# Two transformer blocks on one core: the rounded half of every weight tile is written by ScalarE instead of GpSimd

## The chip, the cores and the metric

The kernel runs on one core of a Trainium2 chip. The metric is the device time of one execution in microseconds (us); the time of a kernel is the median of several runs. The engines are TensorE (PE in the profile; PEld is its loading of weights), VectorE (DVE), ScalarE (ACT), GpSimd (POOL) and SyncE (SP), which here issues most of the DMA transfers.

## The reference

The input `x` is 1 x 1024 tokens x 1024 channels in fp32. Two blocks follow each other:

```python
# block 1
h = rms_norm(x, norm1_g)
q, k, v, g_ret, u, g_s5 = split(h @ w_in)
ret = retention(rotary(q), rotary(k), v) * silu(g_ret)     # 8 heads, chunks of 128
ssm = s5_branch(u) * silu(g_s5)      # linear recurrence, gelu, then
                                     # y * sigmoid(y @ glu_w + glu_b)   (the GLU)
x = x + concat(ret, ssm) @ w_out
x = x + cross_attention(rms_norm(x), rms_norm(mem)) @ xa_wo   # 256 memory tokens
x = rms_norm(x, norm_f_g)
# block 2
p = rmsnorm(x) @ w_in_2
x = x + concat(sgu, short_conv, delta_rule, gla)(p) @ w_out_2
x = x + (silu(h @ w_gate) * (h @ w_up)) @ w_down       # h = rmsnorm(x), 2816 hidden
out = rmsnorm(x, final_norm_w_2)
```

All of it must have fp32 accuracy.

## The kernel before

**Split operands.** TensorE multiplies in a rounded format (`float32r`). To keep fp32 accuracy each operand a is held as two tiles: `hi`, which is a rounded to that format, and `lo` = a − hi, exact. A product of two matrices is then three matmuls into the same PSUM accumulator (`mm3`, L187 to L189): hi·hi, hi·lo and lo·hi. So every weight tile that comes from memory must be split before TensorE can use it, and every activation too.

**A weight tile** is 128 input channels x 8 k-tiles x 128 output columns, seen by an engine as 128 partitions x 1024 elements, 512 KB. `weights()` (L169) issues its DMA on SP into `wraw` (three buffers), writes `whi` (four buffers) and then `wlo` (four buffers). `wlo` on VectorE (L182) reads `wraw` and `whi`, so it always follows the rounding. 204 tiles go this way. Activations are split by `split()` (L164): hi always on ScalarE (L166), lo on VectorE or GpSimd (L167).

**The projections.** `gproj()` (L191) walks over the output tiles of a projection. For each it multiplies 8 k-tiles x 3 matmuls = 24 matmuls of 128 x 512 into one of three PSUM buffers (`mm`), and then calls `evac`, which takes the result from PSUM. With one tile to a group the weights are loaded two tiles ahead. What `evac` does differs by stage; much of it is on ScalarE.

**Stages that the change's neighbours are in** (us of the span of the profiled execution):
- 0 to 110: the start. The memory is normalized, its keys and values are projected and written to DRAM (`ka_d`, `va_d`, through ScalarE copies `mo`, L166), and x is turned and normalized.
- 194 to 303: the S5 inputs. For each of 8 channel tiles four complex products are made; in each, one product is on VectorE and one (`m`, L1398) on GpSimd, and VectorE adds the two (`W`, `E`, L1403). TensorE transposes W (L1422). Projections run beside it.
- 318 to 350: the retention of block 1 begins; ScalarE issues a DMA that fills a DRAM buffer with zeros (`t_d`, L1116), then goes on taking results of projections from PSUM (`g` L480, `sg` L1141).
- 690 to 812: the S5 outputs go to DRAM and come back turned (`oy` L1095, `y_d`).
- 837 to 935: the GLU's projection. `evac` of one tile is a chain through four engines (quoted below); its buffers `sig`, `yt` and `yo` exist once each, so the next tile's L557 and L555 wait for this tile's L560.
- 1214 to 1300: the first block's last two norms beside the last projection. Squares are summed on GpSimd (`ssq`, L274; the squares `sq` come from ScalarE), and TensorE's column sum `ms` (L280) waits for them; GpSimd also scales x (L995) and splits (L311).
- 1950 to 2500: gate/up and down projections of the SwiGLU. Gate and up are done by Winograd's seven products, whose weights are sums and differences of weight tiles, split in `prep()` (L768). There the rounding is on ScalarE for the first pair of tiles and on GpSimd for the other 21.

```python
# evac of the GLU (L555 to L561, shortened)
nc.scalar.activation(sig, ps, AF.Sigmoid, bias=gb[:, ct:ct + 1])      # L555
nc.gpsimd.tensor_add(t, y[0][:, ct], y[1][:, ct])                     # L557  yt
nc.gpsimd.tensor_mul(t, t, sg)                                        # L558  yt
nc.vector.tensor_mul(o, t, sig)                                       # L560  yo
self.split(dst[0][:, ct], dst[1][:, ct], o)                           # L166 ACT, L167 DVE
```

**What sets the order.** The program is built with `tile.TileContext(nc, schedule_with_timeline_sim=True)` (L2211): a scheduler decides by its own model of times in which order each engine's instructions stand in its queue; an engine then runs its queue strictly in that order. Only SP in the start stage and TensorE in the early part of gate/up keep the order of the code.

## Time and profile before

| what | value |
|---|---|
| median of 3 runs | 2550.29 us |
| lowest, highest run | 2542.23, 2551.26 us |
| profiled execution, first to last instruction (span) | 2543.1 us |
| profiled execution, its own time outside of the profile | not listed apart; its span lies 0.9 us above the fastest run |
| mean granted TensorE clock of the profiled execution | 0.985 |

The profile is of one execution. A time in it stands in us from the span's start. Since its span lies at the fastest of the three runs, and two of the runs took 8 to 9 us more, a change that is read from the profile is to be added to the median as a difference.

### The profile page before, as it was taken

How to read it: one execution, taken by the hardware profiler on the slowest of the kernel's cores; microseconds unless marked ns; L12 is line 12 of the kernel's file. 1: busy time of each engine (PE TensorE's matmuls, PEld its weight loads, DVE VectorE, ACT ScalarE, POOL GpSimd, SP SyncE). 2: the span in 40 equal slices, each digit the busy share in tenths (PEclk: the TensorE clock that was granted, in tenths of full speed). 3: DMA queues.
4: the chain of work that ended last, by engine and by line, in shares of the span. 5: the costliest groups of instructions: out<-in, count | busy, mean ns of one | idle time of the engine just before them, and what ended most of it. 6: DMA issues, size and time to landing. Idle time of an engine off the chain costs nothing.

```text
span 2543.1 us, 34912 instructions
## 1 busy us (share of the span) xinstructions
PE 2432.7 (96%) x13241; PEld 2030.9 (80%) x13241; DVE 1589.5 (63%) x2722; ACT 553.2 (22%) x981; POOL 1021.7 (40%) x905
## 2 busy tenths in 40 slices
PE   7998889999999989999999999999989999999998
PEld 7886679999977768888777688977868888888886
DVE  6456669934523765544776653357688766667777
ACT  4223300000001211233343211144240101010002
POOL 4226513423411676436855632145454433321002
PEclk9999999999999999999999999999999999999999
DMA  8745462112697343553336464246243222234222
GB/s 246 222 98 159 149 121 67 60 43 82 214 297 215 119 124 113 169 182 100 93 112 193 132 182 140 83 135 217 82 132 109 92 79 88 84 105 177 99 100 83
DMA packets 421383, 336.81 MB, mean 132 GB/s; under 512 B 46848, under 2 KB 364752, under 8 KB 420384
## 3 DMA queue, kind: packets, MB, share of 16 engines
q1 hardware_dynamic: 378960, 291.05, 37.5%
q10 hardware_dynamic: 42256, 43.52, 6.0%
q8 instruction: 105, 1.72, 0.3%
q14 instruction: 62, 0.51, 0.1%
HBM read 239.00 MB, written 95.52 MB: 132 GB/s over the span
## 4 chain that ended last, share of the span: by engine, by line
PE 73%; POOL 8%; DVE 7%; DMA 5%; issue 5%; SPq 1%; ACT 1%; ACTq 1%; POOLq 0%; DVEq 0%
PE mm L187 18%; PE mm L189 17%; PE mm L188 17%; PE qkv L187 3%; PE qkv L188 2%; PE qkv L189 2%; POOL m L1398 2%; POOL whi L181 1%; PE yps L1089 1%; POOL yt L558 1%; POOL yt L557 1%; POOL ssq L274 1%; PE yps L1085 1%; DVE wlo L182 1%; DMA y<-y_d 1%
## 5 line engine op out<-in xcount | busy, mean ns | idle before, releaser
L187 PE MATMUL mm<-s,whi 128*128 128x512 f32 (+1 forms) x2112 | 837.7, 399 | 28.5 <-ACT sg L1141 9.3
L189 PE MATMUL mm<-s,wlo 128*128 128x512 f32 (+1 forms) x2112 | 829.5, 393 | 5.4 <-DVE wlo L773 4.9
L188 PE MATMUL mm<-s,whi 128*128 128x512 f32 (+1 forms) x2112 | 828.8, 393 | 3.6 <-POOL s L311 2.0
L187 PEld LDWEIGHTS mm<-s,whi 128*128 128x128 f32 x2112 | 402.8, 191 | 121.1 <-issue 17.5
L181 POOL TENSOR_SCALAR whi<-wraw 128x1024 fp32r<-128x1024 f32 x204 | 248.7, 1222 | 618.3 <-PE mm L188 318.0
L189 PEld LDWEIGHTS mm<-s,wlo 128*128 128x128 f32 x2112 | 403.1, 191 | 90.8 <-DVE wlo L773 6.4
L188 PEld LDWEIGHTS mm<-s,whi 128*128 128x128 f32 x2112 | 403.6, 191 | 84.8 <-POOL s L311 3.7
L182 DVE TENSOR_TENSOR wlo<-wraw,whi 128x1024 fp32r<-128x1024 f32 x204 | 297.6, 1461 | 127.7 <-POOL whi L181 126.8
L868 DVE TENSOR_TENSOR s<-mm,s 128x512 f32<-128x512 f32 x176 | 117.4, 686 | 67.0 <-PE mm L189 66.9
L187 PE MATMUL mm<-whi,s 128*128 128x512 f32 (+1 forms) x416 | 155.3, 373 | 1.5 <-DVE mo L167 1.5
L188 PE MATMUL mm<-wlo,s 128*128 128x512 f32 (+1 forms) x416 | 155.1, 373 | 0.5 <-DVE wlo L182 0.5
L189 PE MATMUL mm<-whi,s 128*128 128x512 f32 (+1 forms) x416 | 154.5, 373 | 0.0
L187 PE MATMUL qkv<-whi,s 128*128 128x256 f32 x512 | 151.5, 296 | 0.0
L188 PE MATMUL qkv<-wlo,s 128*128 128x256 f32 x512 | 147.1, 288 | 0.0
L189 PE MATMUL qkv<-whi,s 128*128 128x256 f32 x512 | 146.9, 287 | 0.0
L274 POOL TENSOR_TENSOR ssq<-ssq,sq 128x512 f32<-128x512 f32 x56 | 91.3, 1641 | 28.2 <-ACT sq L273 27.4
L770 POOL TENSOR_SCALAR whi<-wraw 128x1024 fp32r<-128x1024 f32 (+1 forms) x60 | 59.1, 988 | 108.2 <-PE mm L188 79.7
L187 PEld LDWEIGHTS qkv<-whi,s 128*128 128x128 f32 x512 | 97.3, 190 | 4.7 <-issue 3.9
L289 POOL TENSOR_TENSOR rs<-rv,mhalf 128x4 f32<-128x4 f32 (+3 forms) x47 | 52.3, 1115 | 114.2 <-DVE rv L287 113.8
L188 PEld LDWEIGHTS qkv<-wlo,s 128*128 128x128 f32 x512 | 97.4, 190 | 0.9
L189 PEld LDWEIGHTS qkv<-whi,s 128*128 128x128 f32 x512 | 97.4, 190 | 0.3
L739 POOL TENSOR_TENSOR c<-c,c 128x512 f32<-128x512 f32 x44 | 64.3, 1463 | 72.4 <-DVE c L754 43.9
(503 smaller groups left out, 3887.0 us busy)
## 6 DMA issues: line engine op xcount, KB each, us to landing
wraw<-in_w_in_dram SPq DMA_DIRECT2D x58, 512.0 KB
wraw<-in_w_out_dram SPq DMA_DIRECT2D x48, 512.0 KB
wraw<-in_w_gate_up_dram SPq DMA_DIRECT2D x48, 512.0 KB
ff_d<-c SPq DMA_DIRECT2D x44, 256.0 KB
fraw<-ff_d SPq DMA_DIRECT2D x22, 512.0 KB
wraw<-in_w_down_dram SPq DMA_DIRECT2D x22, 512.0 KB
s<-ret_d SPq DMA_DIRECT2D x16, 512.0 KB
s<-x_d SPq DMA_DIRECT2D x16, 512.0 KB
```

Source lines behind the costliest of these rows:

```text
L181: nc.gpsimd.tensor_scalar(hi, raw, 1.0, 0.0, op0=ALU.mult, op1=ALU.add)
L182: nc.vector.tensor_sub(lo, raw, hi.bitcast(F32))
L187: mm(ps, ah, bh, start=start, stop=False)
L188: mm(ps, ah, bl, start=False, stop=False)
L189: mm(ps, al, bh, start=False, stop=stop)
L274: self.nc.gpsimd.tensor_add(ssq, ssq, t)
L289: nc.gpsimd.tensor_tensor(r, v, self.mhalf[:, :1].to_broadcast([P, n]), op=ALU.pow)
L557: nc.gpsimd.tensor_add(t.rearrange("p t c -> p (t c)"), y[0][:, ct].bitcast(F32), y[1][:, ct].bitcast(F32))
L739: g.tensor_mul(src, src, sg[n])
L770: g.tensor_scalar(d[0][:, s], src, 1.0, 0.0, op0=ALU.mult, op1=ALU.add)
L868: v.tensor_add(x, ps, x)
L1398: eng.tensor_tensor(out, a, b, op=ALU.mult)
```

## The change

Three places that rounded a weight tile on GpSimd with `tensor_scalar` (x 1.0 + 0.0) now round it on ScalarE with an `activation` of the function Copy: `weights()` (204 instructions, 128x1024), the inner `split` of `prep()` (102 instructions that were on GpSimd: 39 of 128x1024, 63 of 128x512) and `small_weights()` (1 instruction). Together 307 instructions go from GpSimd's queue to ScalarE's. The lo halves stay on VectorE, and no DMA, matmul or buffer is added or removed. Comments were deleted too, and since three lines of `prep()` go, lines behind L770 carry a number smaller by 3.

```diff
@@ weights()
         hi = self.wp.tile([P, nk, ncol], F32R, tag="whi", name=self.nm("whi"), bufs=4)
         lo = self.wp.tile([P, nk, ncol], F32R, tag="wlo", name=self.nm("wlo"), bufs=4)
-        nc.gpsimd.tensor_scalar(hi, raw, 1.0, 0.0, op0=ALU.mult, op1=ALU.add)
+        nc.scalar.activation(hi, raw, AF.Copy)
         nc.vector.tensor_sub(lo, raw, hi.bitcast(F32))
@@ prep(), inner split
-                if i:
-                    g.tensor_scalar(d[0][:, s], src, 1.0, 0.0, op0=ALU.mult, op1=ALU.add)
-                else:
-                    act.activation(d[0][:, s], src, AF.Copy)
+                act.activation(d[0][:, s], src, AF.Copy)
                 v.tensor_sub(d[1][:, s], src, d[0][:, s].bitcast(F32))
@@ small_weights()
-        nc.gpsimd.tensor_scalar(hi, raw, 1.0, 0.0, op0=ALU.mult, op1=ALU.add)
+        nc.scalar.activation(hi, raw, AF.Copy)
         nc.vector.tensor_sub(lo, raw, hi.bitcast(F32))
```

GpSimd's queue in the GLU's projection, before. A row is the line, the operation, what it writes and reads, and its shape; `s` and `sgl` are the two halves and the gate of the S5 output.

```order
L557 TENSOR_TENSOR yt_8501<-s_1333_7970 128x512
L181 TENSOR_SCALAR whi_8552<-wraw_8550 128x1024
L558 TENSOR_TENSOR yt_8501<-yt_8501,sgl_8497 128x512
L557 TENSOR_TENSOR yt_8543<-s_1333_7970 128x512
L558 TENSOR_TENSOR yt_8543<-yt_8543,sgl_8539 128x512
L181 TENSOR_SCALAR whi_8594<-wraw_8592 128x1024
L557 TENSOR_TENSOR yt_8585<-s_1333_7970 128x512
L558 TENSOR_TENSOR yt_8585<-yt_8585,sgl_8581 128x512
```

The same piece of the changed kernel holds the L557 and L558 of these tiles alone. Here is ScalarE's queue in the same place, of the changed kernel:

```order
L166 ACTIVATE s_1348_8116<-yo_8449 128x512
L181 ACTIVATE whi_8552<-wraw_8550 128x1024
L555 ACTIVATE sig_8499<-mm_8472,glub 128x512
L166 ACTIVATE s_1413_8453<-yo_8504 128x512
L181 ACTIVATE whi_8594<-wraw_8592 128x1024
L555 ACTIVATE sig_8541<-mm_8514,glub 128x512
L166 ACTIVATE s_1413_8453<-yo_8546 128x512
L181 ACTIVATE whi_8636<-wraw_8634 128x1024
```

Each rounding now stands between the split of one tile's result (L166) and the sigmoid of the next (L555), which followed each other directly before.

The second place is ScalarE's queue where the retention of block 1 begins, before; `g` and `sg` empty PSUM accumulators of projections, `t_d` is the DMA of zeros.

```order
L480 ACTIVATE g_2910<-mm_2885 128x512
L151 DMA consts_3468<-in_consts_dram 128x1708
L1116 DMA t_d<-zero 4096x1x129 x2
L480 ACTIVATE g_2938<-mm_2913 128x512
L358 ACTIVATE rsn<-sr_3488 128x256
L359 ACTIVATE sk_3487<-sr_3488 128x256
L1141 ACTIVATE sg_3540<-mm_3515 128x512
```

And of the changed kernel:

```order
L480 ACTIVATE g_2910<-mm_2885 128x512
L151 DMA consts_3468<-in_consts_dram 128x1708
L1113 DMA t_d<-zero 4096x1x129 x2
L181 ACTIVATE whi_3633<-wraw_3630 128x1024
L480 ACTIVATE g_2938<-mm_2913 128x512
L358 ACTIVATE rsn<-sr_3488 128x256
L359 ACTIVATE sk_3487<-sr_3488 128x256
L181 ACTIVATE whi_3639<-wraw_3637 128x1024
L1138 ACTIVATE sg_3540<-mm_3515 128x512
```

One rounding now stands behind the DMA of zeros and ahead of `g_2938`, and another ahead of the first `sg`.

## Rows read from the trace of the kernel before

**Rows 1.** busy us, share of the span and instructions, by engine.
```profile
PE 2432.7 (96%) x13241; PEld 2030.9 (80%) x13241; DVE 1589.5 (63%) x2722; ACT 553.2 (22%) x981; POOL 1021.7 (40%) x905
```

**Rows 2.** groups by line on GpSimd: busy us, mean ns | idle before <-releaser.
```profile
L181 POOL TENSOR_SCALAR whi<-wraw 128x1024 fp32r<-128x1024 f32 x204 | 248.7, 1222 | 618.3 <-PE mm L188 318.0 <-DVE s L868 107.3 <-PE mm L189 70.5
```

**Rows 3.** the same view on ScalarE.
```profile
L166 ACT ACTIVATE s<-fraw 128x1024 fp32r<-128x1024 f32 x22 | 22.1, 1055 | 190.5 <-PE mm L188 177.6 <-DMA s<-xk_d 10.9 <-PE mm L189 2.1
```

**Rows 4.** what TensorE waited for: total us, times, longest us.
```profile
PE wtr L1422 <- DVE W L1403: 16.8, 10, 3.5
PE mm L187 <- ACT sg L1141: 9.3, 1, 9.3
...
PE ms L280 <- POOL ssq L274: 5.1, 3, 4.2
```

**Rows 5.** stretches: busy us (instructions) per engine, granted clock, DMA share, GB/s.
```profile
840.00:930.00 90.00, 83.07 (x355) 65.50 (x354) 66.52 (x43) 16.92 (x28) 68.17 (x43) 1.00 0.40 122
950.00:1000.00 50.00, 50.00 (x230) 41.66 (x229) 27.28 (x27) 9.47 (x15) 29.62 (x20) 1.00 0.27 80
1250.00:1300.00 50.00, 41.07 (x177) 32.10 (x176) 34.24 (x46) 20.82 (x33) 35.89 (x34) 0.93 0.38 103
1950.00:2000.00 50.00, 50.00 (x222) 41.43 (x221) 38.52 (x47) 4.82 (x8) 23.97 (x22) 1.00 0.33 103
```

**Rows 6.** timeline, GpSimd, GLU stage: start, us, instruction [idle before it].
```profile
865.24 2.12 POOL L557 TENSOR_TENSOR yt<-s 128x512 f32<-128x512 f32 x1 [1.07 <-DVE yo L560]
867.44 1.96 POOL L558 TENSOR_TENSOR yt<-yt,sgl 128x512 f32<-128x512 f32 x1
869.36 1.05 POOL L181 TENSOR_SCALAR whi<-wraw 128x1024 fp32r<-128x1024 f32 x1
871.50 2.10 POOL L557 TENSOR_TENSOR yt<-s 128x512 f32<-128x512 f32 x1 [1.08 <-DVE yo L560]
```

**Rows 7.** timeline of VectorE, the same stretch.
```profile
865.00 1.20 DVE L182 TENSOR_TENSOR wlo<-wraw,whi 128x1024 fp32r<-128x1024 f32 x1
866.14 1.77 DVE L167 TENSOR_TENSOR s<-yo,s 128x512 fp32r<-128x512 f32 x1
869.43 1.99 DVE L560 TENSOR_TENSOR yo<-yt,sig 128x512 f32<-128x512 f32 x1 [1.52 <-POOL yt L558]
```

**Rows 8.** L557 from 846 to 935: min/median/max ns, first to last start us.
```profile
L557 POOL TENSOR_TENSOR yt<-s x14: 1274/2100/2717, 846.6 to 927.0; 128x512 f32<-128x512 f32 x14
```

**Rows 9.** timeline of GpSimd in the stage of the S5 inputs.
```profile
244.00 1.06 POOL L181 TENSOR_SCALAR whi<-wraw 128x1024 fp32r<-128x1024 f32 x1
245.68 2.33 POOL L1398 TENSOR_TENSOR m<-PwT,Cr 128x512 f32<-128x512 f32 x1 [0.62 <-DVE E L1403]
249.77 2.32 POOL L1398 TENSOR_TENSOR m<-PreT,Bi 128x512 f32<-128x512 f32 x1 [1.76 <-DVE E L1403]
252.90 2.36 POOL L1398 TENSOR_TENSOR m<-PreT,Br 128x512 f32<-128x512 f32 x1 [0.81 <-DVE W L1403]
```

**Rows 10.** timeline of VectorE, the same stretch.
```profile
244.07 1.52 DVE L1403 TENSOR_TENSOR E<-m,m 128x512 f32<-128x512 f32 x1 [1.02 <-POOL m L1398]
...
246.65 2.44 DVE L182 TENSOR_TENSOR wlo<-wraw,whi 128x1024 fp32r<-128x1024 f32 x1
249.02 0.68 DVE L1403 TENSOR_TENSOR E<-m,m 128x512 f32<-128x512 f32 x1
```

**Rows 11.** all instructions of L181 in 1214 to 1262.
```profile
L181 POOL TENSOR_SCALAR whi<-wraw x6: 1047/1061/2037, 1213.2 to 1257.8; 128x1024 fp32r<-128x1024 f32 x6
```

**Rows 12.** all instructions of L181 in 194 to 303.
```profile
L181 POOL TENSOR_SCALAR whi<-wraw x5: 1043/1050/1057, 202.9 to 291.9; 128x1024 fp32r<-128x1024 f32 x5
```

**Rows 13.** what ScalarE waited for, over the whole span.
```profile
ACT oy L1095 <- DMA y_d<-oy: 47.8, 5, 16.4
```

**Rows 14.** what ScalarE waited for in the start stage, 0 to 110.
```profile
ACT mo L166 <- DMA va_d<-mo: 16.7, 4, 8.0
```

**Rows 15.** timeline of ScalarE where the first block's retention begins.
```profile
318.32 13.04 ACTq L1116 DMA_DIRECT2D t_d<-zero  x2
```

## Prediction

> **What bounds the kernel now.** I read the busy times first. TensorE is busy for 2432.7 of 2543.1 us, 96%; VectorE has 63%, GpSimd 40%, ScalarE 22% [rows 1]. No change on another engine can give back more than the remaining 110.4 us, and it gives back only what stands in TensorE's waits. ScalarE is the emptiest engine, but that is an average; what counts is whether GpSimd's roundings stand in a chain that TensorE waits for, and whether they will do less harm in ScalarE's queue.
>
> So I went next to TensorE's waits and to the table of stretches. In 950 to 1000 and in 1950 to 2000 TensorE has no idle time, 50.00 of 50.00 us [rows 5]: in such stretches (most of the projections, all of gate/up) weights arrive early enough, and where they are rounded is worth nothing unless it becomes late. TensorE falls short in 840 to 930 (83.07 of 90.00), in 1250 to 1300 (41.07 of 50.00, granted clock 0.93) and in the S5 inputs, where its largest wait is for W, 16.8 us in ten waits [rows 4, 5]. In these three stages GpSimd is in the chain. There I read the timelines.
>
> **The price of one rounding.** On GpSimd the 204 of weights() take 1222 ns on average [rows 2]. On ScalarE the same copy of the same shape is already there, for activations: 1055 ns [rows 3]. This price is hardly in doubt. All 307 at 1055 ns at most are 324 us, so ScalarE goes from 553 to at most 877 us, a third of the span. The share bounds nothing; the position in the queue may.
>
> **The GLU stage (840 to 930).** The starts of L557 run from 846.6 to 927.0 in 14 instances [rows 8], so a tile takes (927.0 − 846.6)/13 = 6.18 us. TensorE's 24 matmuls need 24 x 50.00/230 = 5.2 us by the stretch 950 to 1000, and 24 x 50.00/222 = 5.4 by the stretch 1950 to 2000 [rows 5]. So the chain of evac sets the pace. One cycle goes from 865.24 to 871.50, 6.26 us [rows 6]. In it L557 takes 2.12 us and L558 1.96, though the fastest L557 takes 1.27 [rows 8]: each is long where VectorE runs wlo (865.00, 1.20 us) or L167 (866.14, 1.77) beside it. Then the rounding runs at 869.36 for 1.05 us, L560 starts at 869.43 and takes 1.99, and L557 waits 1.08 us for it [rows 6, 7]. L560 thus stretches beside the rounding, and the chain L557, L558, L560 gets longer by the rounding although the rounding is not in it. Without it the cycle is 6.26 − 1.05 = 5.2 us, less than TensorE's 5.4; so TensorE becomes the bound. I take 5.55, since the two are close and wlo still falls at different places in the chain: 13 x (6.18 − 5.55) = 8.2 us saved. Bounds: 10 (13 x 0.77, TensorE alone bounds), and 4, if wlo, arriving at other times, takes half of it back.
>
> On ScalarE the rounding stands between L166 and L555 here. L555 of the next tile is needed only when L557 and L558 are through, about 4.2 us after the last L560 (865.24 to 869.43); L166, rounding and L555 are at most 3 x 1.055 = 3.2 us. It is hidden by 1 us; without that cover it would cost up to 1.05 us a tile, the whole gain.
>
> The Trainium skill ("SBUF — State Buffer", section "Who interferes with whom") says that a VectorE instruction with two SBUF inputs and a GpSimd instruction that reads SBUF exclude each other for their whole length, while ScalarE waits on nobody. The stretched L557 beside wlo and L560 beside the rounding agree. It also speaks against part of the change: wlo, which stays, goes on excluding GpSimd's products and sums. By it the S5 stage below gets back 4.2 us; if the whole excess of its steps were the rounding's, it would be 9, and the sum about 5 us more.
>
> **The S5 inputs (194 to 303).** Five roundings lie there [rows 12]. The step from one GpSimd product to the next takes 3.13 us without one (249.77 to 252.90), and 4.09 in the step before it (245.68 to 249.77) [rows 9]. The rounding at 244.00 lies beside VectorE's E, which takes 1.52 us instead of 0.68; then the wlo that follows it takes 2.44 us ahead of the next E [rows 10]. The first part, 0.84 us, goes with the rounding: 5 x 0.84 = 4.2 us saved. The second, 4.09 − 3.13 = 0.96 us, is wlo's and stays. Bounds: 5 x (0.84 + 0.96) = 9 if wlo then finds a gap; 0 if TensorE's other work there is the end. I take 4.
>
> **The last norms of block 1 (1214 to 1300).** Six roundings lie on GpSimd from 1213.2 to 1257.8, five of about 1.06 us and one of up to 2.04, 7.3 us in all [rows 11], in a queue whose sums TensorE then waits for: ms on ssq, 5.1 us in three waits, the longest 4.2 [rows 4]. Without them the sums are ready up to 7 us earlier, and that wait goes. I take 5. Bounds: 9 (all of TensorE's idle time in 1250 to 1300, 50.00 − 41.07), and 2, since the squares come from ScalarE, which now has the roundings in its queue.
>
> **Elsewhere.** Of the 110.4 us of idle time 6.9, 16.8 and 8.9 are in these three, so 78 are left, spread over many waits. Some may have a rounding in them; I take 3 us saved, bounds 8 saved and 3 lost. The moved sums of gate/up lie in a stretch where TensorE is full [rows 5]: nothing, as long as it stays so.
>
> **What it adds.** Where the retention begins, ScalarE is held by the DMA of zeros for 13.04 us [rows 15], and TensorE already waits 9.3 us for the sg behind it [rows 4]. The order puts one rounding between the DMA and g, another ahead of sg. The one ahead of sg lengthens that wait: about 1 us, at most 2 x 1.055. Taking results from PSUM elsewhere: an accumulator's evacuation comes at most 1.06 us later, where there are three accumulators of 5.2 us each; hidden, but I allow 1 us (0 to 5) for places where it isn't.
>
> **The sum.** −8.2 − 4.2 − 5 − 3 + 1 + 1 = −18.4 us. On the profiled execution 2543.1 becomes 2524.7. Its span lies 7.2 below the median of the three runs, and I apply the difference to the median: 2550.3 − 18.4 = 2532. All bounds on the good side: 10 + 9 + 9 + 8 = 36 saved, 2514; all on the bad side: 4 + 0 + 2 saved, 3 + 2 + 5 lost, 4 lost in all, 2554.
>
> **Rivals.** *B: little comes of it.* The chains get shorter, but what stands next takes over: wlo on VectorE, later now because ScalarE reaches the rounding later, collides with L557, L558 and the norms' sums as before. For it: all of these stages have wlo in the stretched cycles [rows 7, 10], and VectorE has 66.52 of 90.00 us in the GLU stage [rows 5]. Against it: the sum of a cycle's turns is smaller by 1.05 us whatever their order. It gives the lower bounds of the GLU and the norms, 4 + 2, and nothing else: 2550.3 − 6 = 2544.
>
> *C: slower, because ScalarE's queue stands still at times.* Where ScalarE waits for a DMA or issues a long one, roundings behind it in its queue wait too, then wlo, then TensorE. GpSimd had no such waits ahead of weights. The rows for it: 47.8 us in five waits for y_d at L1095, up to 16.4 each [rows 13]; 16.7 us in four for va_d at the start, up to 8.0 [rows 14]; 13.04 us at the DMA of zeros [rows 15]; together 77.5 us. Against it: weights are loaded two tiles ahead, 2 x 5.2 us at full pace, so a wait of under 10 us reaches nothing, and most of these are shorter. It decides where more than 18.4 + 12.8 = 31 of the 77.5 us reach TensorE; if half do, 39 us, the time is 2550.3 − 18.4 + 39 = 2571.
>
> **How the numbers follow.** My forecast has 0.59, B 0.26, C 0.13; 0.02 are left for a larger gain. The predicted time is the forecast's, 2532; its own range is 2514 to 2541. The range of 8 in 10 takes in B and the bounds of the unknown costs, and leaves out C beyond them: 2511 to 2556. A measurement of this kernel tells about 0.5% from no change: below 2537.5 is faster, above 2563.0 slower. Faster has most of the forecast and of the larger gain, and a little of B: 0.58. Same has the rest of these and some of C: 0.29. Slower is C's: 0.13.
>
> **What the profile after would show.** The GLU right: L557 starts 5.4 to 5.7 us apart, L560 near 1.1 us where it took 1.99, TensorE above 86 of 90 us. Wrong: a cycle still near 6.1, with L560 waiting for sig (L555) or L558 beside wlo. The S5 inputs: no E of 1.5 us; steps around a wlo of about 4.1 once, not twice. The norms: the wait of ms on ssq under 1 us; wrong if ssq then waits for sq on ScalarE. The price: L181 on ScalarE at 1.05 us. C would show as TensorE waiting for whi or wlo L182 for several us around the start, 318 to 350 or 700 to 812; that, and a TensorE no longer full in gate/up, would make the prediction wrong.

## The result and the profile after

| | before | after |
|---|---|---|
| median of 4 runs | 2550.61 us (2542.23 to 2551.26) | 2519.44 us (2516.63 to 2520.53) |
| span of the profiled execution | 2543.1 us | 2518.4 us |
| ratio of the times | | 0.989 (95% interval 0.9873 to 0.9906) |

The kernel is 1.1% faster (1.2% by the quotient of the two medians), and the time lies in the range, 2511 to 2556. The spans differ by 24.7 us where the sum of the prediction was 18.4. The rest of the distance from 2532 to 2519 lies in the time that the prediction started from. In every run listed, the time is 1.7 to 2.2 us above the run's own span, mostly 1.8. So the profiled execution of the kernel before, with its span of 2543.1 us, took about 2545 us by this estimate; it was not as fast as the fastest of the three runs (2542.23), as I had read it. In the runs of later comparisons the kernel before had medians of 2543.9 to 2546.9 us, between 2539.7 and 2551.3.

The busy times of the changed kernel, by engine, answer to [rows 1]:

```profile
PE 2427.8 (96%) x13241; PEld 2031.9 (81%) x13241; DVE 1517.8 (60%) x2722; ACT 828.7 (33%) x1289; POOL 679.6 (27%) x598
```

ScalarE has risen from 553 to 829 us, GpSimd has fallen from 1022 to 680. VectorE, which lost no instruction, fell from 1590 to 1518: that is work that used to stretch beside GpSimd's. TensorE's largest waits now (total us, times, longest; the "..." stands for rows in between) answer to [rows 4]:

```profile
PE wtr L1419 <- DVE W L1400: 9.5, 5, 2.6
PE mm L187 <- ACT sg L1138: 8.5, 1, 8.5
...
PE ms L280 <- POOL ssq L274: 4.4, 1, 4.4
PE yps L1082 <- DMA s<-ret_d: 4.1, 1, 4.1
```

The wait for W has fallen from 16.8 us to 9.5. Those for sg and for ms, 9.3 and 5.1 before, are nearly there still, and the one for the S5 output (yps) has grown from 1.6 to 4.1.

Where the 24.7 us lie is best seen from TensorE's progress. Both traces hold the same 13241 matmuls; I compare the start of the n-th in one with that of the n-th in the other. The lead over the kernel before, in us (a minus is a lag), worked out from the traces, for the changed kernel and for the experiments told below. At 4700 and 7700 the orders differ, so that the n-th is not the same multiplication in every kernel and the lead is rough; in all other columns it is the same one.

| n-th matmul (before: at us) | 800 (144) | 1700 (305) | 2000 (368) | 4400 (708) | 4700 (761) | 5000 (813) | 5600 (966) | 7100 (1280) | 7700 (1412) | 8000 (1487) | 10100 (1810) | 10700 (1956) | 13100 (2500) |
|---|---|---|---|---|---|---|---|---|---|---|---|---|---|
| the changed kernel | 2.8 | 6.7 | 5.4 | 5.4 | 0.6 | 0.5 | 14.9 | 14.9 | 14.2 | 19.9 | 20.7 | 24.8 | 24.8 |
| glu_act | 1.6 | 1.8 | 0.7 | 0.7 | −1.4 | −1.4 | 6.9 | 4.6 | 4.6 | 7.3 | 7.4 | 8.2 | 8.2 |
| glu_dve | −0.8 | 1.1 | 0.5 | 0.5 | 0.4 | 0.4 | 3.6 | 1.6 | 1.6 | 2.2 | 4.4 | 5.2 | 4.7 |
| glu_wout | −0.5 | 1.2 | 1.2 | 1.2 | 1.8 | 1.8 | 14.6 | 12.3 | 12.3 | 13.0 | 13.8 | 15.1 | 15.1 |
| gate_act | 0.2 | 2.4 | 3.2 | 3.2 | 3.0 | 3.0 | 3.5 | 1.0 | 1.1 | 0.9 | −0.9 | 0.3 | 0.3 |
| prep_only | −0.3 | −1.5 | −0.3 | −0.3 | −0.2 | −0.2 | −0.5 | 0.0 | 0.0 | −1.4 | −3.5 | −0.2 | −0.2 |
| start_pool | −0.3 | 3.5 | 4.9 | 4.9 | 6.9 | 5.7 | 19.0 | 20.2 | 18.0 | 23.9 | 22.1 | 23.3 | 23.3 |
| b2_pool | 0.8 | 7.4 | 8.8 | 8.7 | 7.0 | 6.8 | 20.3 | 21.2 | 22.6 | 23.7 | 26.5 | 28.6 | 28.6 |
| ret_pool | 2.4 | 7.8 | 8.2 | 8.2 | 4.3 | 4.3 | 16.5 | 17.6 | 15.4 | 22.4 | 18.9 | 23.0 | 23.0 |
| td_sync | 2.4 | 7.9 | −2.4 | −2.4 | −2.6 | −2.7 | 11.0 | 11.0 | 10.3 | 15.9 | 16.2 | 20.1 | 20.1 |
| norm_dve | 2.0 | 7.5 | 5.5 | 5.5 | 0.8 | 0.6 | 15.0 | 20.6 | 25.9 | 33.9 | 33.1 | 37.0 | 37.0 |
| norm_s5loads | 2.6 | 6.3 | 7.9 | 7.8 | 9.9 | 8.3 | 23.0 | 27.0 | 32.3 | 38.8 | 39.0 | 43.3 | 43.0 |
| norm_ret | 2.6 | 6.4 | 7.6 | 7.6 | 6.3 | 6.3 | 19.9 | 23.9 | 29.2 | 36.1 | 32.2 | 36.4 | 36.4 |

The first line is a staircase. It rises in the start (2.8 us), the S5 inputs (3.9), the GLU and what follows it (14.4), the delta rule (5.7) and the beginning of gate/up (4.1); it falls where the retention begins (1.3) and at the S5 outputs (4.8); at the norms of block 1, before 7100, it is flat. Each line compares two single executions, and two things besides the engine of a rounding move it. One is the order that the scheduler makes. Ahead of its edit an experiment has, on every engine, the order of the kernel that it starts from, and behind it as a rule another: glu_act, glu_dve and glu_wout have the kernel before's up to about 800 us, prep_only up to 1900; norm_dve has the changed kernel's up to 1205 us, b2_pool up to 1223, and td_sync has it to the end but for the DMA that it moves. The other is the execution itself. With one and the same order the first four lie between −1.5 and 1.8 up to the 5000th matmul, prep_only is 3.5 behind at the 10100th, and from the 4400th to the 5000th the changed kernel and norm_dve lose 4.9, b2_pool 1.9 and td_sync 0.3. So a step of up to some 4 us in one trace says little by itself; below it is set beside the same step in the other traces.

### The profile page after: what moved, and what is told of

It reads as the page before. It is cut to its first block, busy times and chain, and to the rows that moved or that the text cites. A ratio compares the mean times of both kernels' runs of the same rounds, so it can differ in the third digit from the quotient of the medians.

```text
span 2518.4 us, 34817 instructions
## 1 busy us (share of the span) xinstructions
PE 2427.8 (96%) x13241; PEld 2031.9 (81%) x13241; DVE 1517.8 (60%) x2722; ACT 828.7 (33%) x1289; POOL 679.6 (27%) x598
## 4 chain that ended last, share of the span: by engine, by line
PE 80%; DVE 5%; POOL 5%; DMA 3%; issue 2%; ACT 2%; SPq 1%; ACTq 1%; POOLq 0%; DVEq 0%
PE mm L187 20%; PE mm L188 20%; PE mm L189 20%; PE qkv L187 3%; PE qkv L188 2%; PE qkv L189 2%; POOL m L1395 2%; PE yps L1086 1%; PE yps L1082 1%; POOL s L992 1%; POOL ssq L274 1%; DVE s L167 1%; PE dz L2132 1%; PE gob L1710 1%; DMA s<-ret_d 1%
## 5 line engine op out<-in xcount | busy, mean ns | idle before, releaser
L182 DVE TENSOR_TENSOR wlo<-wraw,whi 128x1024 fp32r<-128x1024 f32 x204 | 282.6, 1387 | 188.5 <-ACT whi L181 183.7
L181 ACT ACTIVATE whi<-wraw 128x1024 fp32r<-128x1024 f32 x204 | 214.7, 1056 | 369.5 <-PE mm L188 218.0
L865 DVE TENSOR_TENSOR s<-mm,s 128x512 f32<-128x512 f32 x176 | 118.3, 688 | 66.6 <-PE mm L189 66.6
L769 ACT ACTIVATE whi<-wraw 128x1024 fp32r<-128x1024 f32 (+1 forms) x62 | 55.7, 907 | 139.3 <-PE mm L188 68.0
L512 DVE TENSOR_TENSOR s<-mm,s 128x512 f32<-128x512 f32 x32 | 22.0, 688 | 113.9 <-PE mm L189 113.8
```

What stands on the lines that cost most here:

```text
L181: nc.scalar.activation(hi, raw, AF.Copy)
L182: nc.vector.tensor_sub(lo, raw, hi.bitcast(F32))
L769: act.activation(d[0][:, s], src, AF.Copy)
L865: v.tensor_add(x, ps, x)
```

## Experiments

In all of them `weights()` takes the engine of the rounding from its caller (`on="a"` is ScalarE, `"g"` GpSimd, `"v"` VectorE). Those that start from the kernel before keep GpSimd everywhere else.

**glu_act: only the GLU on ScalarE.**

```diff
@@ the kernel before, glu()
-  return self.gproj(I["s5_glu_w"][0], list(range(KD)), {h: y}, [h], evac)
+  return self.gproj(I["s5_glu_w"][0], list(range(KD)), {h: y}, [h], evac, on="a")
```

> The kernel before, with the rounding on ScalarE only in the GLU's projection (16 of the 307). Theory (GpSimd's turn in the evac chain sets the GLU's pace): the cycle of L557 falls from 6.18 to about 5.6 us, the stage gives back about 14 us as it did in the changed kernel (from -0.5 to -14.9 us between TensorE's 5000th and 5600th matmul), so the span is about 2529 instead of 2543.1. Rival (the gain came with the new order of the whole program, not with this stage): cycle above 6 us, span within 4 us of 2543.

Measured: 2536.89 us, ratio 0.9967 (0.9952 to 0.9982), span 2534.9. The starts of L557 (minimum/median/maximum ns, first and last start):

```profile
L557 POOL TENSOR_TENSOR yt<-s x15: 1293/1297/3251, 842.1 to 921.2; 128x512 f32<-128x512 f32 x15
```

(921.2 − 842.1)/14 is 5.65 us a tile. Between the 5000th and the 5600th matmul the kernel gains 8.3 us (from −1.4 to 6.9). So the stage gains with no other stage changed, but 8 us and not the 14 that I now expected; 8.2 was the term of the prediction.

**glu_wout: the GLU and the projection behind it.**

```diff
@@ the kernel before, glu()
-  return self.gproj(I["s5_glu_w"][0], list(range(KD)), {h: y}, [h], evac)
+  return self.gproj(I["s5_glu_w"][0], list(range(KD)), {h: y}, [h], evac, on="a")
@@ behind it
-  self.proj(w_out[D:2 * D], list(range(KD)), ssm, [0], evac)
-  self.late(self.gproj(w_out[D:2 * D], list(range(KD)), ssm, [1], evac), norm2(0, 1), 4, 0.5)
+  self.proj(w_out[D:2 * D], list(range(KD)), ssm, [0], evac, on="a")
+  self.late(self.gproj(w_out[D:2 * D], list(range(KD)), ssm, [1], evac, on="a"), norm2(0, 1), 4, 0.5)
```

> The kernel before, with the rounding on ScalarE in the GLU's projection and in the projection behind it (the S5 half of the output projection, 16 tiles more). With the GLU's alone the stage gave back 8.3 us of the 14.4 of the whole change. Theory (the other 6 are where the GLU hands over: two roundings on GpSimd of the next projection still stretch the last tiles' chain, TensorE waits 3.2 us for s L512, and its clock falls): the wait for s L512 is gone, 13 to 15 us are given back between TensorE's 5000th and 5600th matmul, span about 2529. Rival (the 6 us came with the order of the whole program): 8 to 9 us there, span 2534 to 2536.

Measured: 2529.21 us, ratio 0.9935 (0.992 to 0.995), span 2528.4. The gain in the same stretch is 12.8 us (1.8 to 14.6), and TensorE has no wait for s L512 there. Of the other 6 us of the step 4.5 (12.8 − 8.3) are thus the handover, where roundings of the next projection stretch the last tiles. The rest is not told from the spread of this step in the changed kernel and its variants, 12.2 to 14.7. What the handover cost before is seen in TensorE's wait there, and in the 20 us behind the last L557, of the kernel before and of the changed one (stretch, busy us and instructions by engine, granted clock, DMA share, GB/s):

```profile
PE mm L187 <- DVE s L512: 3.2, 1, 3.2
```

```profile
927.00:947.00 20.00, 16.24 (x59) 12.58 (x58) 15.42 (x13) 4.26 (x7) 13.70 (x9) 0.83 0.42 121
```

```profile
917.00:937.00 20.00, 20.00 (x90) 16.57 (x89) 14.02 (x14) 10.26 (x14) 8.06 (x5) 1.00 0.54 158
```

Before, TensorE was busy for 16.24 of 20 us, and the granted clock, 0.83 on average, fell within the wait from 1.00 (2.4 GHz) to 0.50 (1.2 GHz) and stayed there for 6.8 us. After, TensorE has no gap, and the clock stays at 1.00. The prediction had the waits of the evac chain, but not the wait behind the stage, nor the slower clock that came with it.

**glu_dve: the GLU's rounding on VectorE.**

```diff
@@ the kernel before, glu()
-  return self.gproj(I["s5_glu_w"][0], list(range(KD)), {h: y}, [h], evac)
+  return self.gproj(I["s5_glu_w"][0], list(range(KD)), {h: y}, [h], evac, on="v")
@@ weights(), for on="v"
-  nc.gpsimd.tensor_scalar(hi, raw, 1.0, 0.0, op0=ALU.mult, op1=ALU.add)
+  nc.vector.tensor_copy(hi, raw)
```

> The kernel before, with the rounding of the GLU's projection on VectorE. Theory (it is GpSimd's time that the rounding takes, and an instruction of VectorE with one input does not hold GpSimd up): the rounding fits beside L557 or L558, cycle about 5.6, span about 2529 to 2531. Rival (all work of VectorE and GpSimd on these tiles takes turns, so the rounding costs its full time on either): cycle 6.0 to 6.6, span 2540 or more.

Measured: 2541.42 us, ratio 0.9982 (0.9968 to 0.9997), span 2538.4; 3.2 us gained in the stage. The roundings and L557:

```profile
L181 DVE CAST whi<-wraw x12: 685/2126/2167, 835.5 to 902.0; 128x1024 fp32r<-128x1024 f32 x12
```

```profile
L557 POOL TENSOR_TENSOR yt<-s x15: 1269/1297/2118, 839.1 to 924.5; 128x512 f32<-128x512 f32 x15
```

The copy takes 0.685 us at best and 2.126 at the median: it waits its turn behind GpSimd's L557 or L558. L557 starts every (924.5 − 839.1)/14 = 6.10 us. The rival was right on the cycle (6.0 to 6.6); the span, 2538.4, came out 1.6 us below what it said. Between VectorE and GpSimd the rounding's time has to be found whichever has it. On ScalarE it takes 1.06 us beside all of them. The Trainium skill ("SBUF — State Buffer", section "Who interferes with whom") says that a copy on VectorE can run in a mode that takes the pair of ports it shares with GpSimd. This trace agrees in that the copy is held up; the mode itself does not show in it.

**gate_act: only the projection beside the S5 inputs.**

```diff
@@ the kernel before
-  self.weave(self.gproj(w_in, list(range(32, 40)), h1, range(NH), evac_g),
+  self.weave(self.gproj(w_in, list(range(32, 40)), h1, range(NH), evac_g, on="a"),
```

> The kernel before, with the rounding on ScalarE only in the projection beside the S5 inputs (8 tiles, 5 of them between 194 and 303 us). Theory (the rounding stretches VectorE's E or W by 0.84 us each time, and the wlo behind it stays): 3 to 5 us given back between TensorE's 1100th and 1700th matmul, span about 2539, the wlo beside a GpSimd product still near 2.4 us. Rival (wlo then finds a gap): 8 to 9 us. Second rival (the gain there came from the start's order): under 1 us.

Measured: 2541.93 us, ratio 0.9987 (0.9978 to 0.9997), span 2542.3. The lead grows by 2.1 us between the 1100th (0.3) and the 1700th (2.4): less than the 3 to 5 expected, and neither rival's. I had expected five roundings of this stretch to go to ScalarE, but only three did (190 to 305 us):

```profile
L181 ACT ACTIVATE whi<-wraw x3: 1058/1062/1062, 199.9 to 244.2; 128x1024 fp32r<-128x1024 f32 x3
L181 POOL TENSOR_SCALAR whi<-wraw x2: 1044/1048/1052, 267.4 to 291.1; 128x1024 fp32r<-128x1024 f32 x2
```

Beside each of the two that stayed on GpSimd a sum of VectorE still takes 1.52 us, and no other one in this stretch takes over 0.75:

```profile
267.49 1.52 DVE L1400 TENSOR_TENSOR E<-m,m 128x512 f32<-128x512 f32 x1 [1.02 <-POOL m L1395]
291.20 1.52 DVE L1400 TENSOR_TENSOR W<-m,m 128x512 f32<-128x512 f32 x1 [1.30 <-POOL m L1395]
```

Three times 0.84 us are 2.5, near the 2.1 measured. Four of the five wlo there still took 2.43 to 2.47 us. By the end of the trace the gain is gone again in stages that were not touched, above all between the 5600th and the 7100th (3.5 to 1.0); the medians of the runs differ by 3.2 us (2545.11 and 2541.93).

**prep_only: only the sums of gate and up.**

```diff
@@ the kernel before, prep(), inner split
-                if i:
-                    g.tensor_scalar(d[0][:, s], src, 1.0, 0.0, op0=ALU.mult, op1=ALU.add)
-                else:
-                    act.activation(d[0][:, s], src, AF.Copy)
+                act.activation(d[0][:, s], src, AF.Copy)
```

> The kernel before, with only the roundings of prep() (the sums of gate and up, 102 instructions) on ScalarE. Theory (they make the first pairs' weights late where gate/up begins, and nothing later): 3 to 5 us given back between TensorE's 10100th and 10700th matmul, nothing behind it, span about 2539. Rival (these 4 us came from weights() or from the order of the stages ahead of it): less than 1 us there, span 2541 to 2545.

Measured: 2539.54 us, ratio 0.9984 (0.9973 to 0.9994), span 2543.3. Between the 10100th and the 10700th matmul it gains 3.3 us, where the changed kernel gains 4.1; behind that, nothing. The same amount was lost ahead of it, between the 7700th and the 10100th, where the order is still that of the kernel before: that loss is a difference between two executions, and so the span did not move. The medians of the runs differ by 4.3 us (2543.88 and 2539.54).

**start_pool: the start back on GpSimd.**

```diff
@@ the changed kernel, memory_kv()
-  given = {ct: self.weights([wk[:, ct * P:(ct + 1) * P]], KD) for ct in range(3)}
+  given = {ct: self.weights([wk[:, ct * P:(ct + 1) * P]], KD, on="g") for ct in range(3)}
...
-                            n=MEM, given=given):
+                            n=MEM, given=given, on="g"):
...
-  ws = [self.weights([wv[k * 512:(k + 1) * 512, c * 256:(c + 1) * 256]], 4) for k in range(2)]
+  ws = [self.weights([wv[k * 512:(k + 1) * 512, c * 256:(c + 1) * 256]], 4, on="g") for k in range(2)]
@@ stage1()
-  u_proj = self.gproj(w_in, list(range(24, 32)), h1, range(NH), evac_u, group=4)
+  u_proj = self.gproj(w_in, list(range(24, 32)), h1, range(NH), evac_u, group=4, on="g")
```

> The changed kernel, with the roundings of the start (keys and values of the memory, and the u projection) back on GpSimd. Theory (TensorE's waits for mo and whi there, 6.5 us before and 1.4 after, fell because GpSimd's lo halves of the start no longer stand beside roundings): the 2.8 us given back by the 800th matmul are lost again, span about 2521. Rival (they come from the order alone): 1 us or less is lost there.

Measured: 2520.05 us, ratio 0.9904 (0.9885 to 0.9922), span 2519.9. The 2.8 us are lost again (−0.3 at the 800th). At this matmul the seven kernels with the start's roundings on GpSimd, the kernel before among them, lie between −0.8 and 1.6, the seven with them on ScalarE between 0.8 and 2.8. TensorE's waits in 0 to 110 us for mo, and for a rounding on GpSimd where there is one, of the changed kernel and of start_pool:

```profile
PE mm L187 <- DVE mo L167: 1.4, 1, 1.4
```

```profile
PE mm L187 <- DVE mo L167: 4.8, 3, 3.3
...
PE mm L187 <- POOL whi L181: 1.4, 1, 1.4
```

From 1.4 us they go back to 6.2. But this kernel also loses nothing at the S5 outputs (4.9 to 6.9), so its time is that of the changed kernel. A lead of 5 us is therefore not bound to be given back there.

**b2_pool: the mixers of block 2 back on GpSimd.**

```diff
@@ the changed kernel, here and in the other weights() and gproj() of the mixers
-  return self.k.gproj(self.w[:, c0:c0 + n * P], list(range(n)), self.h, range(NH), evac)
+  return self.k.gproj(self.w[:, c0:c0 + n * P], list(range(n)), self.h, range(NH), evac, on="g")
@@ small_weights()
-  nc.scalar.activation(hi, raw, AF.Copy)
+  nc.gpsimd.tensor_scalar(hi, raw, 1.0, 0.0, op0=ALU.mult, op1=ALU.add)
```

> The changed kernel, with the roundings of the second block's mixers (all weight tiles from the first projection of block 2 to the SGU) back on GpSimd. Theory (the 5 us given back in the delta rule, between TensorE's 7700th and 8000th matmul, come from GpSimd being free of roundings there): they are lost again, span about 2523. Rival (they come from another order that the scheduler chose, whatever the engine): the 5 us stay, span 2516 to 2520. The norms of block 1 hold three of these roundings; if those matter, up to 3 us more are lost there.

Measured: 2517.52 us, ratio 0.9893 (0.9877 to 0.991), span 2514.6. In the delta rule the lead grows by 1.1 us (22.6 to 23.7) where it grew by 5.7; from the 7100th to the 8000th, both the same multiplication in the two traces, by 2.5 where it grew by 5.0. So half of that step or more does come with the roundings. TensorE's waits in 1385 to 1475 us of the changed kernel, and of b2_pool:

```profile
PE dt L2128 <- ACT s L2123: 3.5, 1, 3.5
PE t1p L2046 <- DVE s L2029: 2.4, 2, 2.1
```

```profile
PE r L2121 <- DVE s L2129: 5.0, 1, 5.0
PE t1p L2046 <- DVE s L2029: 4.6, 2, 2.8
```

3.7 us more. The span did not get longer, and my forecast of it failed: this trace is 5.4 us ahead of the changed kernel's at the 5600th matmul (20.3 and 14.9), where both have the same order, so that lead is the execution's. The ratio, too, is the changed kernel's (0.9893 and 0.989): what the roundings cost in the delta rule does not show in the time of the runs. Nor did the norms lose.

**ret_pool: the retention's half of the output projection back on GpSimd.**

```diff
@@ the changed kernel, ret_part()
-  self.gproj(w_out[0:D], list(range(KD)), {h: (ret[h][:, 0], ret[h][:, 1])}, [h], evac_ret)
+  self.gproj(w_out[0:D], list(range(KD)), {h: (ret[h][:, 0], ret[h][:, 1])}, [h], evac_ret, on="g")
```

> The changed kernel, with the rounding back on GpSimd only for the retention's half of the output projection (16 tiles, 690 to 835 us). Theory (in ScalarE's queue the roundings stand behind DMA issues, and weights come 4 us late at 710): TensorE's wait of 4.1 us there goes below 2, the lead over the kernel before at the 4700th matmul is back from 0.6 to about 5 us, span about 2514 instead of 2518.4. Rival (the DMA engines bound that stretch and give any lead back): lead at the 4700th matmul under 2 us, span 2517 to 2520.

Measured: 2517.14 us, ratio 0.9885 (0.9864 to 0.9906), span 2520.2. TensorE's wait at the S5 outputs:

```profile
PE yps L1082 <- DMA oU<-u_d: 4.0, 1, 4.0
```

It is there as in the changed kernel, 4.0 us, and 3.9 us of lead are lost (8.2 to 4.3). My theory fell: roundings behind DMAs are not what TensorE waits for there.

**norm_dve: one of GpSimd's other tasks in the last norms on VectorE.**

```diff
@@ the changed kernel, norms()
-                g.tensor_mul(x, x, rb)
+                v.tensor_mul(x, x, rb)
```

> The changed kernel, with the scaling of x in the last norms of the first block (L992, 16 instructions) on VectorE instead of GpSimd. Theory (GpSimd's queue, not the squares from ScalarE, makes the sums late there): the wait of ms on ssq falls from 4.4 to below 1.5 us, span about 2514. Rival (the squares are late, since ScalarE now has the roundings): the wait stays at 3 us or more, span 2517 or more. Second rival (VectorE then makes its own results late): the wait moves to DVE s L972 or DVE nt, span 2517 to 2524.

Measured: 2507.92 us, ratio 0.9846 (0.9823 to 0.987), span 2506.2. In the changed kernel GpSimd had, in 1195 to 1250 us (busy us, mean ns | idle before):

```profile
L274 POOL TENSOR_TENSOR ssq<-ssq,sq 128x512 f32<-128x512 f32 x14 | 21.4, 1551 | 2.2 <-ACT sq L273 2.2
L992 POOL TENSOR_TENSOR s<-s,rb 128x512 f32<-128x512 f32 x8 | 14.5, 1823 | 2.1 <-ACT s L991 2.1
L311 POOL TENSOR_TENSOR s<-nt,s 128x512 fp32r<-128x512 f32 x4 | 7.1, 1767 | 0.0
```

These are 43.0 us, and with the rest GpSimd was busy for 46.8 of the 55 us; instructions that take 1.27 to 1.3 us alone take 1.55 to 1.82 here. TensorE's wait for the sums in norm_dve is

```profile
PE ms L280 <- POOL ssq L274: 1.3, 2, 1.2
```

against 4.4 in the changed kernel, and the lead grows by 5.6 us up to the 7100th matmul and by another 5.3 up to the 7700th, where it stood still. In 1200 to 1250 us the engines did, first in the changed kernel, then in norm_dve:

```profile
1200.00:1250.00 50.00, 45.58 (x209) 38.26 (x208) 33.75 (x35) 24.61 (x38) 44.54 (x29) 0.95 0.43 108
```

```profile
1200.00:1250.00 50.00, 48.66 (x224) 40.32 (x223) 38.19 (x56) 25.95 (x40) 34.42 (x26) 0.97 0.45 111
```

So the theory holds: GpSimd's own queue made the sums late, with no rounding left in it. The span fell by 12 us, where I expected 4.

**norm_s5loads: and the loads of the S5 output from GpSimd.**

```diff
@@ norm_dve, s5_output(), load()
-            nc.scalar.dma_start(U8, u_d[gs].rearrange("g s q c -> (s q) g c"))
+            nc.gpsimd.dma_start(U8, u_d[gs].rearrange("g s q c -> (s q) g c"))
...
-            nc.scalar.dma_start(TZ, k_d[ct])
+            nc.gpsimd.dma_start(TZ, k_d[ct])
...
-            nc.scalar.dma_start(E.rearrange("p a b t q -> p (a b t q)"), e_d[ct])
+            nc.gpsimd.dma_start(E.rearrange("p a b t q -> p (a b t q)"), e_d[ct])
```

> The kernel norm_dve, with the loads of the S5 output (oU, TZ, oE, 24 DMAs) issued by GpSimd instead of ScalarE, so that no rounding stands behind them and they do not share ScalarE's DMA queue. Theory (around 700 the loss of about 4.8 us between the 4400th and 4700th matmul comes from ScalarE's queue being held while it issues these loads): loss below 1.5 us there, TensorE's wait for yps below 2 us, span about 2502. Rival (the loads themselves are late, because the DMA engines are full with the retention's results): the wait stays near 4 us, span 2505 to 2508.

Measured: 2500.05 us (2496.9 to 2502.1), ratio 0.9822 (0.9804 to 0.9839), span 2500.2. It is the fastest, 19 us below the changed kernel. ScalarE's queue in the changed kernel (an ACTq row is a DMA being issued):

```profile
698.20 0.92 ACTq L1067 DMA_DIRECT2D oU<-u_d  x1
708.01 0.33 ACTq L1069 DMA_DIRECT2D TZ<-k_d  x1
710.13 0.33 ACTq L1071 DMA_DIRECT2D oE<-e_d  x1
710.56 2.00 ACT L181 ACTIVATE whi<-wraw 128x1024 fp32r<-128x1024 f32 x2 [17.31 <-DMA s<-ret_d]
```

The first six loads begin at 695.14 and are only out at 710.46; between the second oU and its TZ stand 9 us. TensorE's first yps starts right behind the sixth load:

```profile
710.52 1.20 PE L1082 MATMUL yps<-oU,TZ 128*128 128x128 f32 x4 [4.13 <-DMA s<-ret_d]
```

So it does in all twelve traces in which TensorE waits there and ScalarE issues the loads, 0.06 to 0.10 us behind the sixth, the kernel before among them:

```profile
703.22 0.44 ACTq L1070 DMA_DIRECT2D oU<-u_d  x1
...
716.43 0.33 ACTq L1074 DMA_DIRECT2D oE<-e_d  x1
```

```profile
716.85 0.68 PE L1085 MATMUL yps<-oU,TZ 128*128 128x128 f32 x4 [1.65 <-DMA s<-ret_d]
```

GpSimd issues the same six like this (first and last):

```profile
693.41 1.17 POOL L1067 DMA_DIRECT2D oU<-u_d  x1 [3.07 <-DMA ret_d<-glo]
...
697.10 0.53 POOL L1071 DMA_DIRECT2D oE<-e_d  x1
```

They are out in 4.2 us, and what is left of TensorE's wait there is

```profile
PE yps L1082 <- ACT oy L1092: 0.9, 1, 0.9
```

The lead no longer falls (7.8 to 9.9; to the 5000th 8.3). The theory held: TensorE waits until ScalarE has issued the loads, and the two roundings at 710.56 stood behind them without being TensorE's wait. The profile puts the wait down to one of several DMAs (s<-ret_d, oU or oE); what ties it to ScalarE's queue is that it ends with the sixth issue in all twelve traces. But this wait did not come with the change, and its length is not fixed. The kernel before has it too: its six loads take 13.5 us, and TensorE waits 1.6 us. With the changed kernel's order b2_pool and td_sync take 12.7 and 13.1 us, wait 2.0 and 1.9 us, and lose 1.9 and 0.3 us of lead by the 5000th, where the changed kernel takes 15.3, waits 4.1 and loses 4.9. Why ScalarE needs between 9 us (start_pool) and 15 to issue them, no run shows.

**norm_ret: norm_dve with ret_pool.** The edits are those of norm_dve and ret_pool together.

> The kernel norm_dve, with the rounding of the retention's half of the output projection on GpSimd, as in ret_pool. In ret_pool the retention began 2.8 us earlier than in the changed kernel. If that is a gain of its own: span about 2503. If it is lost again further on, as in ret_pool: span 2505 to 2510.

Measured: 2506.45 us, ratio 0.9852 (0.9837 to 0.9867), span 2506.9: as norm_dve. The earlier retention was no gain of this edit: up to 660 us ret_pool and norm_ret have the changed kernel's order, so it came with the execution. What it was ahead is lost again, first by 1.3 us at the S5 outputs and then by 3.9 between the 8000th and the 10100th.

**td_sync: the DMA of zeros issued by SP.**

```diff
@@ the changed kernel, retention()
-            nc.scalar.dma_start(self.t_d[i].rearrange("n h s c -> (n h s c)").rearrange("(p a b) -> p a b", p=P, b=P + 1),
+            nc.sync.dma_start(self.t_d[i].rearrange("n h s c -> (n h s c)").rearrange("(p a b) -> p a b", p=P, b=P + 1),
                                 zero.unsqueeze(1).to_broadcast([P, 32, P + 1]))
```

> The changed kernel, with the DMA of zeros (t_d) issued by SP instead of ScalarE, so that no rounding and no g or sg stands behind its 14.5 us. Theory (the waits of 2.5 us for g and 8.5 us for sg are ScalarE's queue): both go below 1.5 us, 8 to 11 us given back between TensorE's 1400th and 2000th matmul, span about 2509. Rival (sg is late for another reason, since it starts 8 us after the last instruction ahead of it): the wait for g goes, that for sg stays, span 2516. Second rival (SP's queue is then held and weights are late): span 2518 or more.

Measured: 2524.98 us, ratio 0.9926 (0.9911 to 0.9941), span 2523.0. SP's queue where the retention begins, and TensorE's wait for sg:

```profile
309.93 14.46 SPq L1113 DMA_DIRECT2D t_d<-zero  x2
324.44 16.02 SPq L481 DMA_DIRECT2D sg_d<-g  x1
```

```profile
PE mm L187 <- ACT sg L1138: 20.9, 1, 20.9
```

The second rival: now SP is held for 14.46 us by the zeros and for 16.02 more at the store behind them, and the wait for sg is 20.9 us instead of 8.5. So issuing the DMA on SP does not help: it takes 14.46 us there too. Whether the wait for sg of 8.5 us in the changed kernel is ScalarE's queue or something else, this run does not tell, since it made another wait instead. Another queue, or a smaller DMA, was not tried.

## Why the prediction was right, and where not

**The price of a rounding** held: 1056 ns on ScalarE, forecast 1055. All 204 of weights() lie within 33 ns there (shortest, median, longest):

```profile
L181 ACT ACTIVATE whi<-wraw x204: 1037/1060/1070, 8.6 to 2469.4; 128x1024 fp32r<-128x1024 f32 x102
```

ScalarE at 829 us is a third of the span, as bounded.

**The GLU** was right in mechanism, and its term right in size for what it counted. L557 starts, in the changed kernel:

```profile
L557 POOL TENSOR_TENSOR yt<-s x15: 1290/1299/2124, 839.3 to 917.2; 128x512 f32<-128x512 f32 x15
```

That is (917.2 − 839.3)/14 = 5.56 us a tile, forecast 5.55. GpSimd and VectorE in one cycle, to be set beside [rows 6, 7]:

```profile
883.85 1.31 POOL L557 TENSOR_TENSOR yt<-s 128x512 f32<-128x512 f32 x1 [2.22 <-DVE yo L560]
885.24 1.96 POOL L558 TENSOR_TENSOR yt<-yt,sgl 128x512 f32<-128x512 f32 x1
889.44 1.31 POOL L557 TENSOR_TENSOR yt<-s 128x512 f32<-128x512 f32 x1 [2.24 <-DVE yo L560]
```

```profile
882.64 1.13 DVE L560 TENSOR_TENSOR yo<-yt,sig 128x512 f32<-128x512 f32 x1
884.47 1.24 DVE L167 TENSOR_TENSOR s<-yo,s 128x512 fp32r<-128x512 f32 x1 [0.70 <-ACT s L166]
885.63 2.65 DVE L182 TENSOR_TENSOR wlo<-wraw,whi 128x1024 fp32r<-128x1024 f32 x1
888.20 1.16 DVE L560 TENSOR_TENSOR yo<-yt,sig 128x512 f32<-128x512 f32 x1
```

L560 takes 1.13 instead of 1.99 us, as forecast. VectorE's wlo, though, takes 2.65 beside L558, and L560 follows on its end: what I gave as the reason for 5.55 instead of 5.4 is there to see. ScalarE's rounding between L166 and L555 hid: TensorE was busy for 77.00 of 77 us from 840 to 917. glu_act confirms the term alone, 8.3 us against 8.2. Mis-sized is what the stage costs altogether, 14.4: the term stopped at the last L557, and glu_wout shows 12.8 with the projection behind it.

**The S5 inputs**: 3.9 us, forecast 4.2 in the sum ("I take 4" in its own paragraph). GpSimd's steps and VectorE around one wlo in the changed kernel:

```profile
242.65 2.35 POOL L1395 TENSOR_TENSOR m<-PreT,Bi 128x512 f32<-128x512 f32 x1 [0.80 <-DVE E L1400]
246.77 2.33 POOL L1395 TENSOR_TENSOR m<-PreT,Br 128x512 f32<-128x512 f32 x1 [1.76 <-DVE W L1400]
249.90 2.36 POOL L1395 TENSOR_TENSOR m<-PwT,nCi 128x512 f32<-128x512 f32 x1 [0.81 <-DVE W L1400]
```

```profile
243.65 2.44 DVE L182 TENSOR_TENSOR wlo<-wraw,whi 128x1024 fp32r<-128x1024 f32 x1
246.01 0.68 DVE L1400 TENSOR_TENSOR W<-m,m 128x512 f32<-128x512 f32 x1
```

One step of 4.12 us (242.65 to 246.77) remains beside the wlo of 2.44 us, and the next is 3.13 again. The five sums of 1.52 us of the kernel before are gone: none here takes over 0.75. That is what the prediction said would stay and what would go. The wlo starts 1.0 us into a product of GpSimd and ends 1.09 us behind it, where a wlo takes 1.2 us alone. The Trainium skill ("SBUF — State Buffer", section "Who interferes with whom") has the two exclude each other, as the prediction says; this trace agrees. gate_act, with three of the five roundings, gave 2.1 us. The size holds in the other traces too: from the 800th to the 1700th the eight kernels with these roundings on ScalarE gain 3.7 to 6.6 us, the five with all of them on GpSimd, the kernel before among them, −1.2 to 1.9.

**The last norms of block 1** are the step that failed: "I take 5", and nothing came in the changed kernel (0 to 1.2 us in start_pool, ret_pool and td_sync, whose norms are the same), with the wait of ms on ssq at 4.4 us. I counted the 7.3 us of roundings in GpSimd's queue as time by which the sums would be earlier. But GpSimd had 43 us of other work in these 55 us, and norm_dve shows that this is what holds the sums back. It was not the squares from ScalarE, on which my lower bound rested: they are there still in norm_dve.

**Elsewhere** I took 3 us in the lump. The steps were 2.8 (the start, shown by start_pool), 5.7 (the delta rule, half of it or more shown by b2_pool) and 3.3 to 4.1 (gate/up, by prep_only; 1.2 to 4.3 over all kernels with these roundings on ScalarE, 0 to 1.3 over those without), about 12 us. For gate/up I argued that TensorE was full, from a stretch at 1950 us; the weights of the first pairs, before it, were not looked at.

**What it adds**: where the retention begins, 1.3 us, forecast 1; that they agree is chance. ScalarE's queue there:

```profile
311.45 14.48 ACTq L1113 DMA_DIRECT2D t_d<-zero  x2
325.98 1.06 ACT L181 ACTIVATE whi<-wraw 128x1024 fp32r<-128x1024 f32 x1 [16.52 <-PE mm L189]
326.94 0.58 ACT L480 ACTIVATE g<-mm 128x512 f32<-128x512 f32 x1
```

The rounding stands for 1.06 us between the DMA of zeros, 14.48 us, and g, as the order said. But with the same order there norm_dve loses 2.0 us between the 1700th and the 2000th matmul, and b2_pool and norm_s5loads gain 1.4 and 1.6; and the wait for sg, which the prediction had about 1 us longer, fell from 9.3 to 8.5. So no run shows this term, nor the 1 us allowed for PSUM elsewhere. The loss of 4.8 us at the S5 outputs was not in the sum. It lies at a place of rival C, ScalarE's queue behind DMAs, but not by its mechanism: ret_pool took the roundings away, and the wait stayed. In the execution of b2_pool, with the same order, it is 1.9.

**Rival B** has the mechanism of the norms, where GpSimd's other work took over; **rival C** decided nothing. The sum of the terms was 18.4 against 24.7 in the traces: about 6 too little at the GLU's end and 9 elsewhere, 9 to 10 too much in the norms and the S5 outputs. That the sum came as near as it did is luck in part, since these errors cancel. Also, 4.9 of the 24.7 us are not idle time but busy time of TensorE (2432.7 to 2427.8), which the bound of 110.4 us left out. The other 6 us of the miss come from setting the difference against the median of three runs, 2550.3, when the profiled execution took about 2545 and the later medians lay 3 to 6 us lower. Why the kernel before spreads over 11 us is left open.

## What to carry to other kernels

An instruction that is not in a chain can lengthen it, by stretching what runs beside it: look for instructions of VectorE and GpSimd that take longer than their fastest, and give the work to an engine that does not take turns with either. Removing work from a queue that stayed full gave nothing here; add up what else the queue has to do before the thing that is waited for. Count the wait behind a stage too, with the slower clock that may come with it, and compare the progress of TensorE in two traces matmul by matmul: it shows gains and losses by stage that the total hides. Do it with more than one trace of an order, since two executions of one order differed here by up to 5 us in a stage.

## What was not expected of the hardware

A copy of 128x1024 on VectorE took 0.685 us at its shortest and 2.126 at the median in a stage where GpSimd's sums ran beside it (glu_dve), so an instruction with a single input was held up by GpSimd as well. ScalarE took 9 to 15 us to issue six loads of about 0.5 MB each (13.5 in the kernel before, 15.3 in the changed one) that GpSimd's queue issued in 4.2.
